# Three narrow matmuls in place of two wide ones for queries, w_o and the first two FFN pairs of a decoder layer

## The chip, the cores and the metric

One of the cores of a Trainium2 chip runs the whole program. The metric is the device time of one execution in microseconds (us); the time before is the median of three runs. The profile is of one execution, and its times count from the start of its span.

## What is computed

One decoder layer on 256 positions of width 2048, in float32: a Mamba-2 SSD mixer, then cross-attention with 4 heads into 256 memory tokens, then a gated FFN with a causal convolution of 3 taps, each between two RMS norms and added to the residual. What matters here, cut from the reference:

```python
q = (h @ w_q).reshape(bsz, L, XA_HEADS, XA_HEAD_DIM)
k, v = jnp.split(mem_n @ w_kv, 2, axis=-1)
...
s = jnp.einsum('bthd,bmhd->bhtm', q, k).astype(jnp.float32) * (XA_HEAD_DIM ** -0.5)
p = jax.nn.softmax(s, axis=-1).astype(v.dtype)
o = jnp.einsum('bhtm,bmhd->bthd', p, v).reshape(bsz, L, XA_DIM)
return o @ w_o
...
u = _causal_dwconv(h @ w_up, conv_w, conv_b)
gate, val = jnp.split(u, 2, axis=-1)
return (jax.nn.silu(gate) * val) @ w_down
```

## The kernel before

Activations lie transposed: 128 channels on the partitions, 256 positions (T) along the row. A float32 product is made of fp32r matmuls on operands split into a high part (a rounded copy, ScalarE, line 139 for weights) and a low part (the rest, VectorE, line 153 for weights): high by high, high by low, low by high. Weights come in chunks of 128 x 2048 through 3 raw buffers, and are split in halves of 1024 columns into 5 split buffers ("split"); a few halves of the first FFN chunks go into free parts of the tile G.

A product of one 128-column block of weights with an activation goes over 16 steps of 128 channels (4 steps for w_o, whose depth is the 4 heads). A step has two forms:

- narrow, `mm3` (lines 241 to 244): three matmuls of 256 columns into the same 256 columns of a PSUM bank;
- wide, `mm2` (lines 246 to 249): the high weights by high and low activations in one matmul of 512 columns, and the low weights by the high activations into the second half of the bank. The block's result is then the sum of the bank's halves: `folded` (lines 251 to 256) copies the second half to SBUF on ScalarE (line 254) and adds the first on VectorE (line 255).

The SSD input projections (80 blocks) are narrow; all from w_out on is wide. After the SSD output the work is laid out in slots, one or more blocks ("lanes") each, in the order: keys 0 to 3, values 0 to 2, queries 0 to 3, value 3, then w_o (16 blocks; the first four as four lanes of one slot, step by step), then the FFN. A block's bank is emptied by its post function in the next slot (`q_post` line 771, `wo_post` line 877, `fconv` line 904), and hooks put the attention between the steps of the slots after: scores of head h (`s_mm`), softmax (`smax`), transposed probabilities (`p_tr`), product with values (`o_mm`), its split into the high and low parts that w_o reads (`o_post`). The tiles q, p and pT have one buffer each, so a head waits for the head before. Banks named pj rotate through four.

`wo_post` squares a block for the third norm, scales it into m, and adds the square to a running sum. When w_o is done, `chain3` (line 983) takes the norm: `pe1` (line 300, matmuls with ones), a power on GpSimd, `pe2` (line 320, transposes), then the residual and the high and low parts of H, which the FFN reads. The first FFN slot has four lanes (gate 0, value 0, gate 1, value 1, in two banks pj and the banks pt and py); their posts are kept ("late") until the fourth norm's row rb is copied (line 328), in the next slot.

The instructions are issued through a scheduler that reorders them on each engine; `hot` raises a post's priority, and `pinned` keeps chain3 in its written order (line 53).

Of the kernel before, what the change touches and what calls it, by code (L numbers as in the profile page):

```python
# [7 lines left out]
F32 = mybir.dt.float32  # L8
FR = mybir.dt.float32r
I32 = mybir.dt.int32  # L10
AF = mybir.ActivationFunctionType
OP = mybir.AluOpType

T = 256
DM = 2048
KD = DM // 128
# [6 lines left out]
NF = FH // 128  # L23
# [38 lines left out]
def hybrid_layer_kernel(ctx, tc, xT, memT, pvd, alog, w_dt, w_in, w_kv, w_q, w_out, w_o, w_up, w_dn, out):  # L62
    nc = tc.nc
    V, S, P, PE = nc.vector, nc.scalar, nc.gpsimd, nc.tensor
# [11 lines left out]
    m = consts.tile([128, KD, T], F32, name="m")  # L76
# [9 lines left out]
    def col(name, j):  # L86
        return pv[:, PV[name] + j:PV[name] + j + 1]
# [4 lines left out]
    B = {}  # L92
# [106 lines left out]
    def hot(fn):  # L199

        def steps(g):
            while True:
                with tc.high_priority():
                    if next(g, g) is g:
                        return
                yield

        def f(*args):
            with tc.high_priority():
                g = fn(*args)  # L210
            return steps(g) if hasattr(g, "__next__") else g
        return f
# [5 lines left out]
    slots = []  # L218

    def new_chunk(src, n, kind="w"):  # L220
        chunks.append((src, n, kind))
        return len(chunks) - 1

    def slot():
        slots.append(Slot())
        return len(slots) - 1
# [3 lines left out]
    def sl(i):  # L230
        return hooked.setdefault(i, Slot())

    def add_block(src, n, mov, post, lane_of=None):

        s = slot() if lane_of is None else lane_of
        c = new_chunk(src, n)
        slots[s].lanes.append((c, 0, mov, post, None, True))
        return s


# [10 lines left out]
    def folded(ps, pool, name, bufs):  # L251

        t = pool.tile([128, T], F32, name=name, bufs=bufs)
        S.activation(t, ps[:, T:], AF.Copy)  # L254
        V.tensor_tensor(t, ps[:, :T], t, op=OP.add)  # L255
        return t

    def hilo(dst, src, scale=None):

        hi, lo = dst  # L260
        if scale is None:
            S.activation(hi, src, AF.Copy)  # L262
            yield
            return V.tensor_tensor(lo, src, hi.bitcast(F32), op=OP.subtract)  # L264
        else:
            S.activation(hi, src, AF.Copy, scale=scale)
            yield
            return V.scalar_tensor_tensor(lo, src, scale, hi.bitcast(F32), op0=OP.mult, op1=OP.subtract)
# [5 lines left out]
    def halves(t):  # L274
        return t[:, 0:T], t[:, T:2 * T]
# [73 lines left out]
    movG = [G[:, k] for k in range(GS)]  # L349
    movH = [H[:, k] for k in range(KD)]  # L350
# [278 lines left out]
    for kind, i in order:  # L629
        s = pos[kind, i]  # L630
        if kind in ("C", "B"):
            blk = 32 + (8 if kind == "C" else 0) + i
# [113 lines left out]
    def v_post(h):  # L746
        def post(ps):
            wB = B["wB"]
            t = folded(ps, wB, "ev", 2)
            V.tensor_tensor(t, t, B["nm"].rbc, op=OP.mult)  # L750
            B["vT", h] = t
        return post

    def k_post(h):
        def post(ps):
            t = folded(ps, B["wB"], "ev", 2)
            V.tensor_tensor(t, t, B["nm"].rbc, op=OP.mult)
            yield from hilo(halves(B["K"][:, h]), t)
        return post
# [11 lines left out]
    def q_post(h):  # L771
        def post(ps):
            q = B["wB"].tile([128, 2 * T], FR, name="q", bufs=1)
            yield from hilo(halves(q), folded(ps, B["wB"], "ev", 2))
            B["q", h] = q
        return post

# [66 lines left out]
    at = {}  # L844
    for kind, h in (("k", 0), ("k", 1), ("k", 2), ("k", 3), ("v", 0), ("v", 1), ("v", 2), ("q", 0), ("q", 1), ("q", 2), ("q", 3), ("v", 3)):
        if kind == "k":
            at[kind, h] = add_block(w_kv[h], 2048, movH, k_post(h))
        elif kind == "v":
            at[kind, h] = add_block(w_kv[XH + h], 2048, movH, v_post(h))
        else:  # L850
            at[kind, h] = add_block(w_q[h], 2048, movG, q_post(h))
    s_k0, s_q0, s_wo = at["k", 0], at["q", 0], max(at.values()) + 1

    hook(s_k0, "pe", lambda: B["nm"].pe1(), 2)
# [11 lines left out]
    for h in range(XH):  # L866
        s = at["q", h]
# [9 lines left out]
    def wo_post(j):  # L877
        def post(ps):
            wB = B["wB"]
            sq = wB.tile([128, T], F32, name="accB" if j == 0 else "sqB", bufs=2 if j else 1)  # L880
            if j == 0:
                B["n3"] = Norm(wB, DM)
            t = folded(ps, wB, "ev", 2)
            B["hold_s"] = S.activation(sq, t, AF.Square)
            S.activation(m[:, j], t, AF.Copy, scale=col("post", KD + j))
            yield
            B["hold_v"] = B["n3"].add(sq, last=j == KD - 1) or B.get("hold_v")
        return post
# [8 lines left out]
    for j in range(KD):  # L897
        if j % 4 == 0:
            c = new_chunk(w_o[j // 4], 2048)
        s = s_wo if 0 < j < 4 else slot()  # L900
        slots[s].lanes.append((c, 4 * (j % 4), MovO(), hot(wo_post(j)), None, True))


    def fconv(ps, blk, dst_name, silu):
        wB = B["wB"]
        t = folded(ps, wB, "ev", 2)
        V.tensor_tensor(t, t, B["n4"].rbc, op=OP.mult)
        u = wB.tile([128, T], F32, name="fu", bufs=2)
        w = PV["fw"] + 3 * blk
        S.activation(u, t, AF.Identity, bias=col("fb", blk), scale=pv[:, w + 2:w + 3])  # L910
        yield
        for j in (1, 0):
            d = 2 - j
            V.scalar_tensor_tensor(u[:, d:], t[:, :T - d], pv[:, w + j:w + j + 1], u[:, d:],  # L914
                                   op0=OP.mult, op1=OP.add)
        if silu:
            s = wB.tile([128, T], F32, name="sg", bufs=2)
            S.activation(s, u, AF.Silu)
            return s
        return u  # L920

    def gate_post(f):
        def post(ps):
            B["gate", f] = yield from fconv(ps, f, "sg", True)
        return post

    def val_post(f):
        def post(ps):
            u = yield from fconv(ps, NF + f, "uv", False)
            V.tensor_tensor(u, u, B.pop(("gate", f)), op=OP.mult)  # L930
            yield from hilo(halves(G[:, f % GS]), u)
        return post
# [20 lines left out]
    up_no = 0  # L953
    first_up = len(slots)

    def add_up(f):
        nonlocal up_no
        if f < 2:
            if f == 0:
                slot()  # L960
                B["late"] = []
                in_g.update({len(chunks): 0, len(chunks) + 1: 1})
                c = len(chunks)
                held.update(range(c, c + 4))
                for i, (dc, h) in enumerate(((0, 0), (0, 1), (1, 0), (2, 0), (3, 0), (1, 1), (2, 1), (3, 1))):
                    moved[c + i // 2, i % 2] = (c + dc, h)
            add_block(w_up[up_no], 2048, movH, lambda ps: B["late"].append((gate_post(f), ps)), lane_of=first_up)
            add_block(w_up[up_no + 1], 2048, movH, lambda ps: B["late"].append((val_post(f), ps)), lane_of=first_up)
        else:
            add_block(w_up[up_no], 2048, movH, gate_post(f))  # L970
            add_block(w_up[up_no + 1], 2048, movH, val_post(f))
        up_no += 2
# [3 lines left out]
    for si, (f0, f1) in enumerate(SETS):  # L976
        while done < min(f1 + 1, NF):
            add_up(done)
            done += 1
        for j in range(KD):  # L980
            add_block(w_dn[si][j], (f1 - f0) * 128, [G[:, f % GS] for f in range(f0, f1)], dn_post(si, j))
# [62 lines left out]
    for i, s in enumerate(slots):  # L1044
# [29 lines left out]
        for k in range(nk):  # L1074
            for ln, ps in zip(lanes, pss):
# [4 lines left out]
                c, off, mov = ln[0], ln[1], ln[2]  # L1080
# [5 lines left out]
                n = len(mov)  # L1086
# [15 lines left out]
    n5, wB = B["n5"], B["wB"]  # L1102
# [99 lines left out]
```

## Time and profile before

| | |
|---|---|
| median of 3 runs | 1584.14 us (1583.5 to 1584.51) |
| the profiled execution: its own time | 1584.14 us |
| its span, first to last instruction | 1582.4 us |
| TensorE (PE) busy | 1543.2 us, 98% |
| VectorE (DVE) busy | 1213.8 us, 77% |
| ScalarE (ACT) busy | 975.9 us, 62% |
| mean granted TensorE clock | 0.991 |

PE is busy in nearly all of the 40 slices of the span; two slices around 780 and 820 us are at 8 and 6 tenths. Matmuls are pipelined and overlap in the records, so what one costs is read from the distance of starts, not from its length. The profile's rows name a line, an engine, an operation, the tile written and the tiles read, and in brackets the idle time before it and what ended it.

### The profile page before, as it was taken

The numbers are of one execution on the slowest core, as the hardware profiler recorded it, in microseconds if no ns is written. First come the engines' busy times: TensorE is split into PE (matmuls) and PEld (weight loads), VectorE is DVE, ScalarE is ACT, GpSimd is POOL, SyncE is SP. The second block draws the span as 40 slices with busy tenths as digits, with TensorE's granted clock in tenths as the row PEclk, the third lists the DMA queues.
The fourth block names the chain that finished last, engine by engine and source line by source line (L and its number), as shares of the span: only waits on it lengthen the run. The fifth ranks groups of instructions, "written<-read, shape, count | busy, mean of one in ns | idle before, by whom it ended". The sixth has DMA issues, their size and how long they took to land.

```text
span 1582.4 us, 25562 instructions
## 1 busy us (share of the span) xinstructions
PE 1543.2 (98%) x10104; PEld 1406.7 (89%) x10104; DVE 1213.8 (77%) x1942; ACT 975.9 (62%) x1603; POOL 7.9 (0%) x14
## 2 busy tenths in 40 slices
PE   8999999999999999999869999999999999999997
PEld 7999999889999999888758788888888888888886
DVE  7799988746898897869578878755877765778775
ACT  6798887645777765756575655544555533555553
POOL 0000000000000000000000000000000000000000
PEclk9999999999999999999989999999999999999999
DMA  7665555554555445754334455555555555555452
GB/s 266 222 219 191 178 194 189 187 195 166 205 180 183 170 160 188 291 177 169 106 107 171 171 191 186 178 197 188 193 195 193 180 186 195 188 190 195 155 208 77
DMA packets 47289, 292.08 MB, mean 185 GB/s; under 512 B 5504, under 2 KB 5568, under 8 KB 19776
## 3 DMA queue, kind: packets, MB, share of 16 engines
q1 hardware_dynamic: 46592, 289.60, 52.6%
q8 instruction: 79, 1.29, 0.3%
q10 hardware_dynamic: 576, 0.84, 0.2%
q14 instruction: 42, 0.34, 0.1%
HBM read 288.26 MB, written 2.16 MB: 184 GB/s over the span
## 4 chain that ended last, share of the span: by engine, by line
PE 51%; issue 45%; DVE 2%; ACT 1%; DMA 1%; POOL 0%; SPq 0%; POOLq 0%; DVEq 0%
PE pj L248 12%; PE pj L244 9%; PE pj L243 9%; PE pj L242 9%; PE pj L249 6%; PE py L244 1%; PE py L242 1%; PE py L243 1%; PE pt L534 0%; DMA m<-in_xT_dram 0%; DVE m L1119 0%; PE ms L300 0%; DMA raw<-in_w_up_dram 0%; ACT hi L139 0%; PE pt L248 0%
## 5 line engine op out<-in xcount | busy, mean ns | idle before, releaser
L139 ACT ACTIVATE hi<-raw 128x1024 fp32r<-128x1024 f32 (+2 forms) x518 | 539.7, 1045 | 481.0 <-PE pj L248 399.2
L153 DVE TENSOR_TENSOR lo<-raw,hi 128x1024 fp32r<-128x1024 f32 (+2 forms) x518 | 623.9, 1206 | 260.8 <-ACT hi L139 256.4
L248 PE MATMUL pj<-H,hi 128*128 128x512 f32 x1472 | 513.0, 393 | 3.4 <-DVE ev L255 3.4
L248 PE MATMUL pj<-G,hi 128*128 128x512 f32 x1280 | 444.5, 392 | 0.0
L249 PE MATMUL pj<-H,lo 128*128 128x256 f32 x1472 | 412.2, 280 | 0.0
L242 PE MATMUL pj<-H,hi 128*128 128x256 f32 x1280 | 361.3, 283 | 6.9 <-ACT hi L262 6.6
L244 PE MATMUL pj<-H,lo 128*128 128x256 f32 x1280 | 360.1, 282 | 0.8 <-DVE lo L264 0.7
L243 PE MATMUL pj<-H,hi 128*128 128x256 f32 x1280 | 360.2, 282 | 0.0
L249 PE MATMUL pj<-G,lo 128*128 128x256 f32 x1280 | 356.7, 280 | 0.0
L248 PEld LDWEIGHTS pj<-H,hi 128*128 128x128 f32 x1472 | 277.0, 188 | 64.6 <-issue 3.7
L248 PEld LDWEIGHTS pj<-G,hi 128*128 128x128 f32 x1280 | 239.8, 188 | 52.1
L249 PEld LDWEIGHTS pj<-H,lo 128*128 128x128 f32 x1472 | 277.1, 188 | 0.1
L242 PEld LDWEIGHTS pj<-H,hi 128*128 128x128 f32 x1280 | 241.4, 189 | 8.8 <-ACT hi L262 7.6
L244 PEld LDWEIGHTS pj<-H,lo 128*128 128x128 f32 x1280 | 241.7, 189 | 2.1 <-DVE lo L264 1.6
L243 PEld LDWEIGHTS pj<-H,hi 128*128 128x128 f32 x1280 | 242.0, 189 | 1.0
L249 PEld LDWEIGHTS pj<-G,lo 128*128 128x128 f32 x1280 | 240.4, 188 | 0.6
L914 DVE SCALAR_TENSOR_TENSOR fu<-ev,pv,fu 128x255 f32<-128x255 f32 (+1 forms) x176 | 84.3, 480 | 3.2 <-ACT fu L910 0.3
L456 DVE SCALAR_TENSOR_TENSOR u<-ev,pv,u 128x255 f32<-128x255 f32 (+2 forms) x144 | 68.5, 478 | 5.1 <-ACT u L452 3.9
L910 ACT ACTIVATE fu<-ev,pv 128x256 f32<-128x256 f32 x88 | 51.7, 589 | 1.1 <-DVE G L264 0.9
L255 DVE TENSOR_TENSOR ev<-pj,ev 128x256 f32<-128x256 f32 x113 | 46.6, 418 | 4.3 <-ACT ev L254 4.3
L254 ACT ACTIVATE ev<-pj 128x256 f32<-128x256 f32 x113 | 40.8, 367 | 7.4 <-PE pj L249 4.7
L367 DVE TENSOR_TENSOR ev<-pj,rx 128x256 f32<-128x256 f32 x80 | 33.6, 421 | 13.2 <-PE pj L244 10.4
(254 smaller groups left out, 1246.1 us busy)
## 6 DMA issues: line engine op xcount, KB each, us to landing
raw<-in_w_up_dram SPq DMA_DIRECT2D x88, 1024.0 KB, 4.8
raw<-in_w_in_dram SPq DMA_DIRECT2D x78, 1024.0 KB, 4.8
raw<-in_w_out_dram SPq DMA_DIRECT2D x32, 1024.0 KB, 4.8
raw<-in_w_dn_dram SPq DMA_DIRECT2D x32, 960.0 KB, 4.7
raw<-in_w_dn_dram SPq DMA_DIRECT2D x16, 896.0 KB, 4.6
rows<-rows_d SPq DMA_DIRECT2D x32, 256.0 KB, 3.9
raw<-in_w_kv_dram SPq DMA_DIRECT2D x8, 1024.0 KB, 4.8
raw<-in_w_q_dram SPq DMA_DIRECT2D x4, 1024.0 KB, 4.8
```

The source lines that it names most:

```text
L139: S.activation(hi_t[c, h][:, :b - a], raw_t[c][:, a:b], AF.Copy)
L153: V.tensor_tensor(lo_t[c, h][:, :b - a], raw_t[c][:, a:b], hi_t[c, h][:, :b - a].bitcast(F32), op=OP.subtract)
L242: PE.matmul(ps, whi, xhi, start=start, stop=False)
L243: PE.matmul(ps, whi, xlo, start=False, stop=False)
L244: B["mm"] = PE.matmul(ps, wlo, xhi, start=False, stop=stop)
L248: PE.matmul(ps, whi, x, start=start, stop=False)
L249: B["mm"] = PE.matmul(ps[:, T:], wlo, x[:, 0:T], start=False, stop=stop)
L254: S.activation(t, ps[:, T:], AF.Copy)
L255: V.tensor_tensor(t, ps[:, :T], t, op=OP.add)
L456: V.scalar_tensor_tensor(u[:, d:], ps[:, :T - d], pv[:, w + j:w + j + 1], u[:, d:], op0=OP.mult, op1=OP.add)
L910: S.activation(u, t, AF.Identity, bias=col("fb", blk), scale=pv[:, w + 2:w + 3])
L914: V.scalar_tensor_tensor(u[:, d:], t[:, :T - d], pv[:, w + j:w + j + 1], u[:, d:], op0=OP.mult, op1=OP.add)
```

## The change

Queries, w_o and the first two FFN pairs (gates and values 0 and 1) go back from the wide to the narrow form; keys, values, all other FFN blocks, and the SSD output stay wide. Their posts read the bank directly instead of a folded tile: `q_post` splits it, `wo_post` squares it and scales it (the scaling of every fourth block goes to VectorE), and `fconv` multiplies it by the norm's row.

```diff
-    def add_block(src, n, mov, post, lane_of=None):
+    def add_block(src, n, mov, post, lane_of=None, wide=True):
...
-        slots[s].lanes.append((c, 0, mov, post, None, True))
+        slots[s].lanes.append((c, 0, mov, post, None, wide))
...
-            yield from hilo(halves(q), folded(ps, B["wB"], "ev", 2))
+            yield from hilo(halves(q), ps[:, :T])
...
-            at[kind, h] = add_block(w_q[h], 2048, movG, q_post(h))
+            at[kind, h] = add_block(w_q[h], 2048, movG, q_post(h), wide=False)
...
-            t = folded(ps, wB, "ev", 2)
-            B["hold_s"] = S.activation(sq, t, AF.Square)
-            S.activation(m[:, j], t, AF.Copy, scale=col("post", KD + j))
+            B["hold_s"] = S.activation(sq, ps[:, :T], AF.Square)
+            if j % 4:
+                S.activation(m[:, j], ps[:, :T], AF.Copy, scale=col("post", KD + j))
+            else:
+                V.tensor_scalar(m[:, j], ps[:, :T], col("post", KD + j), None, op0=OP.mult)
...
-        slots[s].lanes.append((c, 4 * (j % 4), MovO(), hot(wo_post(j)), None, True))
+        slots[s].lanes.append((c, 4 * (j % 4), MovO(), hot(wo_post(j)), None, False))
...
-        t = folded(ps, wB, "ev", 2)
-        V.tensor_tensor(t, t, B["n4"].rbc, op=OP.mult)
+        if blk % NF < 2:
+            t = wB.tile([128, T], F32, name="ev", bufs=2)
+            V.tensor_tensor(t, ps[:, :T], B["n4"].rbc, op=OP.mult)
+        else:
+            t = folded(ps, wB, "ev", 2)
+            V.tensor_tensor(t, t, B["n4"].rbc, op=OP.mult)
...
-            add_block(w_up[up_no], 2048, movH, lambda ps: B["late"].append((gate_post(f), ps)), lane_of=first_up)
-            add_block(w_up[up_no + 1], 2048, movH, lambda ps: B["late"].append((val_post(f), ps)), lane_of=first_up)
+            add_block(w_up[up_no], 2048, movH, lambda ps: B["late"].append((gate_post(f), ps)), lane_of=first_up, wide=False)
+            add_block(w_up[up_no + 1], 2048, movH, lambda ps: B["late"].append((val_post(f), ps)), lane_of=first_up, wide=False)
```

The scheduler also orders the engines anew. ScalarE from the first query's split to the first softmax, before (q is a query's split, ev a fold's copy, hi a weight split, p the exponentials):

```order
L262 ACTIVATE q<-ev 128x256
L139 ACTIVATE hi<-raw 128x1024
L254 ACTIVATE ev<-pj 128x256
L139 ACTIVATE hi<-raw 128x1024
L262 ACTIVATE q<-ev 128x256
L139 ACTIVATE hi<-raw 128x1024
L254 ACTIVATE ev<-pj 128x256
L805 ACT_TABLE_LOAD
L805 ACTIVATE p,sm<-py,mx,sr 128x256 x2
```

and now (Vt is the split of a transposed value block, which in the order before stands earlier):

```order
L262 ACTIVATE q<-pj 128x256
L139 ACTIVATE hi<-raw 128x1024
L262 ACTIVATE Vt<-pt 128x256
L139 ACTIVATE hi<-raw 128x1024 x2
L262 ACTIVATE q<-pj 128x256
L262 ACTIVATE Vt<-pt 128x256
L805 ACT_TABLE_LOAD
L805 ACTIVATE p,sm<-py,mx,sr 128x256 x2
```

The copies are gone, and the softmax stands before the fourth value's fold. On PE the scores of head 0 stood behind 9 steps of value 3's block, and now stand in query 3's block, around its sixth to ninth step.

ScalarE at the end of w_o, before (the posts of blocks 13 to 15: the rows of line 53 are those of block 15):

```order
L139 ACTIVATE hi<-raw 128x1024
L884 ACTIVATE sqB<-ev 128x256
L885 ACTIVATE m<-ev,pv 128x256
L254 ACTIVATE ev<-pj 128x256
L139 ACTIVATE hi<-raw 128x1024
L884 ACTIVATE sqB<-ev 128x256
L885 ACTIVATE m<-ev,pv 128x256
L53 ACTIVATE ev<-pj 128x256
L53 ACTIVATE sqB<-ev 128x256
L53 ACTIVATE m<-ev,pv 128x256
```

and now:

```order
L139 ACTIVATE hi<-raw 128x1024
L883 ACTIVATE sqB<-pj 128x256
L885 ACTIVATE m<-pj,pv 128x256
L883 ACTIVATE sqB<-pj 128x256
L885 ACTIVATE m<-pj,pv 128x256
L53 ACTIVATE sqB<-pj 128x256
L53 ACTIVATE m<-pj,pv 128x256
```

A post has two instructions on ScalarE instead of three (one, in every fourth block), nothing waits for VectorE between them, and one weight split now stands behind block 15's post.

VectorE at the late posts of the first two FFN pairs, before (rb is the fourth norm's row, fu the convolution):

```order
L153 TENSOR_TENSOR lo<-raw,hi 128x1024 x3
L328 COPY rb<-ms 128x256
L907 TENSOR_TENSOR ev<-ev,rb 128x256 x2
L153 TENSOR_TENSOR lo<-raw,hi 128x1024
L914 SCALAR_TENSOR_TENSOR fu<-ev,pv,fu 128x255 x2
L914 SCALAR_TENSOR_TENSOR fu<-ev,pv,fu 128x254 x2
L153 TENSOR_TENSOR lo<-raw,hi 128x1024
L930 TENSOR_TENSOR fu<-fu,sg 128x256
L255 TENSOR_TENSOR ev<-pt,ev 128x256
L255 TENSOR_TENSOR ev<-py,ev 128x256
L907 TENSOR_TENSOR ev<-ev,rb 128x256 x2
```

and now:

```order
L153 TENSOR_TENSOR lo<-raw,hi 128x1024 x2
L328 COPY rb<-ms 128x256
L910 TENSOR_TENSOR ev<-pj,rb 128x256 x2
L153 TENSOR_TENSOR lo<-raw,hi 128x1024
L920 SCALAR_TENSOR_TENSOR fu<-ev,pv,fu 128x255 x2
L920 SCALAR_TENSOR_TENSOR fu<-ev,pv,fu 128x254 x2
L910 TENSOR_TENSOR ev<-pt,rb 128x256
L910 TENSOR_TENSOR ev<-py,rb 128x256
```

The two banks pj of pair 0 were emptied by folds ahead of these rows; now they are read only after the copy of rb. The sums of the folds and two weight splits (one ahead of rb, one behind) have left this stretch.

## Rows read from the trace of the kernel before

**Rows 1.** The page, busy time by engine over the span
```profile
PE 1543.2 (98%) x10104; PEld 1406.7 (89%) x10104; DVE 1213.8 (77%) x1942; ACT 975.9 (62%) x1603; POOL 7.9 (0%) x14
```

**Rows 2.** PE's waits, 650 to 860 us: total us, times, longest
```profile
PE ms L300 <- DVE accB L290: 6.8, 1, 6.8
PE pj L248 <- DVE H L53: 3.3, 1, 3.3
PE py L242 <- ACT q L262: 2.7, 1, 2.7
```

**Rows 3.** PE's waits, 845 us to the end
```profile
PE pj L248 <- DVE ev L255: 3.4, 1, 3.4
```

**Rows 4.** Stretches: us, busy PE, PEld, DVE, ACT, POOL, granted clock, DMA share, GB/s
```profile
811.00:826.00 15.00, 2.82 (x11) 2.28 (x11) 10.21 (x21) 8.29 (x17) 1.54 (x1) 0.67 0.41 141
877.00:881.00 4.00, 3.94 (x14) 3.33 (x15) 3.63 (x10) 2.42 (x6) 0.00 (x0) 0.58 0.25 104
```

**Rows 5.** PE's timeline (start us, length us): 13 narrow steps, then 33 wide steps
```profile
28.93 0.28 PE L242 MATMUL pj<-H,hi 128*128 128x256 f32 x1
...
33.56 0.28 PE L242 MATMUL pj<-H,hi 128*128 128x256 f32 x1
...
1000.05 0.39 PE L248 MATMUL pj<-H,hi 128*128 128x512 f32 x1
...
1011.49 0.39 PE L248 MATMUL pj<-H,hi 128*128 128x512 f32 x1
```

**Rows 6.** ACT's timeline: query 0's copy, exponentials of heads 0 and 3
```profile
756.39 0.36 ACT L254 ACTIVATE ev<-pj 128x256 f32<-128x256 f32 x1
...
769.86 0.56 ACT L805 ACTIVATE p<-py,mx,sr 128x256 f32<-128x256 f32 x1
...
782.55 0.56 ACT L805 ACTIVATE p<-ms,mx,sr 128x256 f32<-128x256 f32 x1
```

**Rows 7.** PE's timeline: head 0's scores, w_o, the third norm, the FFN's first matmul
```profile
763.99 0.28 PE L242 MATMUL py<-KT,q 128*128 128x256 f32 x1
...
790.21 0.50 PE L248 MATMUL pj<-KT,hi 128*128 128x512 f32 x1 [0.93 <-DVE KT L264]
...
791.76 0.49 PE L248 MATMUL pj<-KT,hi 128*128 128x512 f32 x1
...
810.64 0.28 PE L249 MATMUL pj<-KT,lo 128*128 128x256 f32 x1
817.75 0.59 PE L300 MATMUL ms<-ones,accB 128*128 128x1 f32 x2 [6.83 <-DVE accB L290]
...
819.40 0.56 PE L300 MATMUL ms<-ones,sqB 128*128 128x1 f32 x2
...
825.90 0.77 PE L248 MATMUL pj<-H,G 128*128 128x512 f32 x1 [3.31 <-DVE H L53]
```

**Rows 8.** Groups by line, 757 to 826 us: xcount, busy us, mean ns
```profile
L885 ACT ACTIVATE m<-ev,pv 128x256 f32<-128x256 f32 x15 | 7.4, 496 | 0.0
L254 ACT ACTIVATE ev<-pj 128x256 f32<-128x256 f32 x19 | 6.4, 370 | 2.2 <-PE pj L249 1.2 <-DVE q L264 1.1
L884 ACT ACTIVATE sqB<-ev 128x256 f32<-128x256 f32 x14 | 5.7, 408 | 2.6 <-DVE ev L255 2.6
```

**Rows 9.** ACT's timeline: block 15's square, the first high part of H
```profile
818.06 0.42 ACT L53 ACTIVATE sqB<-ev 128x256 f32<-128x256 f32 x1 [0.99 <-DVE ev L53]
...
823.54 0.51 ACT L53 ACTIVATE H<-x,pv 128x256 fp32r<-128x256 f32 x1 [3.72 <-DVE x L53]
```

**Rows 10.** DVE's timeline: pair 0 multiplied by rb
```profile
865.00 0.76 DVE L907 TENSOR_TENSOR ev<-ev,rb 128x256 f32<-128x256 f32 x2
```

**Rows 11.** PE's timeline: gate 3's first step, the stall ahead of gate 4, full clock again
```profile
862.18 0.39 PE L248 MATMUL pj<-H,hi 128*128 128x512 f32 x1
...
877.06 0.47 PE L248 MATMUL pj<-H,hi 128*128 128x512 f32 x1 [3.40 <-DVE ev L255]
...
881.13 0.40 PE L248 MATMUL pj<-H,hi 128*128 128x512 f32 x1
```

More of the change, by code (lines that the diff above doesn't have):

```diff
@@ L900, in hybrid_layer_kernel, with fconv @@
         s = s_wo if 0 < j < 4 else slot()
-        slots[s].lanes.append((c, 4 * (j % 4), MovO(), hot(wo_post(j)), None, True))
-    def fconv(ps, blk, dst_name, silu):
+        slots[s].lanes.append((c, 4 * (j % 4), MovO(), hot(wo_post(j)), None, False))
+    def fconv(ps, blk, silu):
         wB = B["wB"]
-        t = folded(ps, wB, "ev", 2)
-        V.tensor_tensor(t, t, B["n4"].rbc, op=OP.mult)
+        if blk % NF < 2:
[4 more added lines that the diff above has]
+            V.tensor_tensor(t, t, B["n4"].rbc, op=OP.mult)
         u = wB.tile([128, T], F32, name="fu", bufs=2)
@@ L923, in post @@
         def post(ps):
-            B["gate", f] = yield from fconv(ps, f, "sg", True)
+            B["gate", f] = yield from fconv(ps, f, True)
         return post
@@ L928, in post @@
         def post(ps):
-            u = yield from fconv(ps, NF + f, "uv", False)
+            u = yield from fconv(ps, NF + f, False)
             V.tensor_tensor(u, u, B.pop(("gate", f)), op=OP.mult)
```

## The prediction
> **What bounds the kernel now.** I read the page's busy times first: PE is busy 98% of the span [rows 1], so elsewhere time comes only from PE work itself. Then PE's waits: the three largest from 650 to 860 us stand around attention, w_o and the third norm [rows 2], and one stands alone in the FFN [rows 3]. The stretch from 811 to 826 us shows what they do: 15 us in which PE works 2.82 [rows 4]. So two questions settle this case: what a narrow step costs on PE, and which of these waits hang on the folds that go.
>
> **Price of a step.** A matmul's length overlaps its neighbours', so starts count. 13 narrow steps take 33.56 - 28.93 = 4.63 us, 0.356 each; 33 wide steps take 1011.49 - 1000.05 = 11.44 us, 0.347 each [rows 5]. A narrow step costs 0.010 us more (0.0095, rounded up). The change makes 4 x 16 steps for queries, 16 x 4 for w_o, and 4 x 16 in the FFN narrow: 192 x 0.010 = **+1.9 us**, all on PE's path. The Trainium skill (TensorE: Matmul & The Clock Gate, "Wait — 56ns, not 53.3ns?") gives a full-clock matmul its columns' time plus some 2.5 ns; by it one more matmul a step would cost 192 x 2.5 ns = 0.5 us, an estimate. The trace's difference is four times that, and the rows decide.
>
> **Queries and attention.** A wide query's way to its scores is a copy on ScalarE, a sum on VectorE, then the split on both, each queued behind weight splits. Query 0's copy starts at 756.39 [rows 6] and head 0's scores only at 763.99 [rows 7], behind 9 steps of value 3. The new order puts the query's split where the copy stood, and the scores into query 3's block: 16 steps earlier, 16 x 0.356 = 5.7 us. PE has work in this stretch anyhow (the rest of the projections), so an earlier head takes time off only if the whole chain of four heads follows. In the order now, I walked it with durations of before. Exponentials of head 0 at 763.6 instead of 769.86, of head 3 at 777.4 instead of 782.55 [rows 6]; then the last head's split, and w_o's fourth step at 785.3 instead of 790.21 [rows 7]. That is 4.9, net of the 0.6 that the queries' narrow steps cost, so 5.5 gross. Several of its hops rest on where PE fits head matmuls between projection steps, so I take **-5.0 us**. The bounds are 0 (heads paced as now, only begun earlier: PE would wait among them instead of ahead of them) and -6.3 (head 0's whole lead kept).
>
> **Posts of w_o.** A block's post now costs ScalarE a copy, a square and a scaling, 370, 408 and 496 ns [rows 8], with VectorE's sum between the first and the second. Starts of neighbours lie some 0.1 closer than these lengths. With the weight splits between them the posts fall behind PE, and banks come free late: 47 steps from 791.76 to the start of the last at about 810.4 [rows 7] take 0.397 each instead of 0.347, 2.4 us too much. Now a post costs ScalarE a square and, in three of four blocks, a scaling: 0.3 + 0.75 x 0.4 = 0.6 us by starts, and the seven weight splits of this stretch add 7 x 0.96 / 16 = 0.42. That is 1.0 us a block against PE's 4 x 0.356 = 1.43. ScalarE keeps up; I leave 0.4 for the first bank: **-2.0 us** (bounds 0 and -2.4).
>
> **The tail.** PE's last w_o matmul starts at 810.64, lasts 0.28, and the third norm's sums wait until 817.75; its last starts at 819.40 [rows 7]. The wait is the backlog: block 15's square runs at 818.06 [rows 9], seven microseconds behind its data. With ScalarE level with PE, the square follows the last matmul by a hop of some 0.2, takes 0.42 [rows 9], and the last sum starts 0.9 behind it (819.40 - 818.06 = 1.3 with the square in it). So 1.6 us from PE's end instead of 819.40 - 810.92 = 8.5: **-6.9 us**. Late next would be the fourth split of FFN weights, which moves behind block 15's post and puts a second low part of 1.2 us ahead of the residual on VectorE; GpSimd's power, which runs at that time (1.54) [rows 4], and the transposes cover it to within some 0.2. Bounds: -3.5 (half the backlog remains) and -7.2.
>
> **The FFN's first matmul.** A wide matmul reads the high and low parts of H together, so it starts at 825.90 [rows 7], though the first high part is there from 823.54 + 0.51 = 824.05 [rows 9]. Four narrow matmuls that need only it can run in that wait. At the half clock (here 1.2 GHz) that PE comes back with, four take about 4 x 0.21: **-0.8 us** (bounds 0 and -1.8).
>
> **The late posts.** Now the folds empty pair 0's banks before rb is known, but two folds, a weight split and more stand ahead of gate 2's fold. So PE stands still for 3.40 us ahead of gate 4, then runs 7 steps in 881.13 - 877.06 = 4.07 us instead of 2.4 [rows 11], at a granted clock of 0.58 [rows 4]: 3.4 + 1.6 = 5.0. In the new order gate 2's fold comes three microseconds earlier by VectorE's durations (two sums, a split, a split's wait), and that stall goes. In its place gate 3 needs a bank that is read only behind rb: PE gets there at 862.18 [rows 11], less one step for the new place of the transposes. Before, rb's first product ran at 865.00 [rows 10] behind a split that is no longer ahead of it. Without that split, transposes at 861.8, copy at 862.3 and product at 862.7 free the bank at 863.2, 1.2 later than PE wants it. Sum **-3.8 us** (bounds +0.5, if rb is as late as now and the clock falls too, and -5.0).
>
> **Sum.** 1.9 - 5.0 - 2.0 - 6.9 - 0.8 - 3.8 = -16.6 us. The profiled execution took 1584.14 us, which is also the median, with 1.7 outside the span. 1584.1 - 16.6 = **1567.5 us**. Everything before query 0 and behind gate 4 keeps its order in kind, and PE its 98%; I cost it at nothing.
>
> **Rivals.**
> - *The heads keep their pace.* One buffer each for q, p and pT ties a head to the one before, and PE's wait for a query's split is only 2.7 us [rows 2]. Without the attention term: 1572.5. For it: the chain is long and has no slack; against it: the softmax of head 0 is moved ahead of value 3's fold. 0.15.
> - *The splits are the backlog, not the folds.* If weight splits and their raw loads hold ScalarE in w_o, half of the tail stays (3.4) and half of w_o's stalls (1): 1572, and 1577 together with the first rival. Against it: ScalarE waited 2.6 us for VectorE's sums at the squares alone [rows 8]. 0.15.
> - *ScalarE becomes w_o's bound: slower.* A bank is read twice now, by square and scaling. The Trainium skill (VectorE: DVE Perf Modes, "Rules for kernel authors") advises for several operations on a matmul's output to copy it to SBUF first, which the change undoes. It decides once posts and splits take more than PE's 1.43 us a block; from there each further 0.1 costs 1.6 over 16 blocks. To use up 16.6 us, a post would need 2.5 us a block, 2.1 without splits, against 0.6; then 1587 to 1590. The copy that reads a bank takes 370 ns, less than the square's 408 from SBUF [rows 8], which speaks against it. 0.04.
> - *More than forecast*, if the clock stays up in places where it now falls, or all bounds meet: 1562. 0.06.
>
> That the narrow form wouldn't be used is excluded by the built order. The forecast itself has 0.60.
>
> **Numbers.** 1567.5 us. The range takes the cases at 1572 and most of the one at 1577, and the lower bounds of single terms: 1563.5 to 1576. 0.2%, about 3.2 us, is what a measurement of this kernel can tell from no change. Faster by more: all cases but the slower rival and a sum where nearly all terms fail: 0.93; within: 0.03; slower: 0.04.
>
> **What would show it.** The wait for the running sum (6.8) under 1.5; exponentials of head 0 some 6 us earlier against the projections; the first FFN matmul narrow and ahead of the low part; no 3.4 wait ahead of gate 4, but one of about 1 ahead of gate 3, for the product with rb. A long wait of PE for ScalarE or VectorE inside w_o, or among the heads, would make it wrong.

## The result and the profile after

The changed kernel takes **1563.98 us** (median; 1563.46 to 1564.14), the kernel before 1583.86 in the same comparison: a ratio of 0.9873, 95% interval 0.9856 to 0.9891. It is faster by 20 us; the time lies 3.5 us below the forecast of 1567.5 and half a microsecond above the lower end of the range, 1563.5 to 1576.

The page of the changed kernel, busy time by engine (the line of [rows 1]):

```profile
PE 1538.6 (99%) x10296; PEld 1413.8 (91%) x10296; DVE 1205.5 (77%) x1922; ACT 967.3 (62%) x1575; POOL 7.9 (1%) x14
```

PE runs 192 matmuls more, is busy 4.6 us less in all, and its share rises to 99%: what went is time in which it stood still or ran slowly. PE's waits from 650 to 860 us, where [rows 2] stood before:

```profile
PE pj L242 <- ACT H L53: 2.7, 1, 2.7
...
PE pj L248 <- DVE ev L910: 1.1, 1, 1.1
PE pj L242 <- ACT KT L262: 0.9, 2, 0.5
PE pj L242 <- DVE mx L802: 0.7, 1, 0.7
...
PE pj L243 <- DVE H L53: 0.5, 1, 0.5
PE pj L242 <- DVE m L887: 0.3, 1, 0.3
```

The wait of 6.8 for the running sum is gone, and so is the 2.7 for a query's split. The wait for H's first high part (2.7) and low part (0.5) is what is left of 3.3; the 1.1 ahead of gate 3 (for the product with rb, L910) is new, and the 3.4 of [rows 3] is not there any more. The first steps of w_o wait twice for the high part of a head's output (the 0.9); from block 4 of w_o on, PE waits once, 0.3.

Two stretches with the columns of [rows 4], around the FFN's first matmul, and from the fourth norm's sums to behind gate 4, whose first step now comes at about 859:

```profile
806.00:816.00 10.00, 7.38 (x38) 7.09 (x39) 9.90 (x20) 6.71 (x12) 0.00 (x0) 0.66 0.39 126
...
840.00:900.00 60.00, 58.93 (x349) 52.02 (x348) 50.96 (x89) 39.25 (x62) 1.54 (x1) 1.00 0.54 183
```

In the second one PE misses only the 1.07 ahead of gate 3, and the clock is full.

PE's timeline, with the places of [rows 7, 11] (start, length, and in brackets the wait ahead): the norm ahead of the queries, head 0's scores, w_o's fourth step and block 4, the last w_o matmul, the third norm's sums, the FFN's first matmul, gate 3:

```profile
700.87 0.28 PE L300 MATMUL ms<-ones,sqB 128*128 128x1 f32 x2
...
757.48 0.28 PE L242 MATMUL py<-KT,q 128*128 128x256 f32 x1
...
783.12 0.38 PE L242 MATMUL pj<-KT,hi 128*128 128x256 f32 x1 [0.47 <-ACT KT L262]
...
785.09 0.39 PE L242 MATMUL pj<-KT,hi 128*128 128x256 f32 x1 [0.28 <-DVE m L887]
...
802.35 0.28 PE L244 MATMUL pj<-KT,lo 128*128 128x256 f32 x1
802.73 0.38 PE L300 MATMUL ms<-ones,accB 128*128 128x1 f32 x2
...
803.57 0.36 PE L300 MATMUL ms<-ones,sqB 128*128 128x1 f32 x2
...
808.14 0.80 PE L242 MATMUL pj<-H,G 128*128 128x256 f32 x2 [2.69 <-ACT H L53]
...
847.77 0.47 PE L248 MATMUL pj<-H,hi 128*128 128x512 f32 x1 [1.07 <-DVE ev L910]
```

ScalarE's timeline, with the places of [rows 6, 9]: query 0's split, now straight from the bank, the exponentials of heads 0 and 3, block 15's square:

```profile
754.80 0.37 ACT L262 ACTIVATE q<-pj 128x256 fp32r<-128x256 f32 x1
...
762.68 0.57 ACT L805 ACTIVATE p<-py,mx,sr 128x256 f32<-128x256 f32 x1
...
776.36 0.56 ACT L805 ACTIVATE p<-ms,mx,sr 128x256 f32<-128x256 f32 x1
...
802.66 0.39 ACT L53 ACTIVATE sqB<-pj 128x256 f32<-128x256 f32 x1 [0.63 <-PE pj L244]
```

Executions differ by up to 1.6 us at the very start. So times are compared behind one row that comes before any changed block, the first residual norm's sums: 700.87 here, and in the kernel before

```profile
700.83 0.28 PE L300 MATMUL ms<-ones,sqB 128*128 128x1 f32 x2
```

Behind that row, in us (the runs are told of below; "end" is the span's):

| kernel | exp. of head 0 | w_o block 4 | last w_o matmul | n3's last sum | first FFN matmul | end |
|---|---|---|---|---|---|---|
| before | 69.03 | 90.93 | 109.81 | 118.57 | 125.07 | 881.57 |
| changed | 61.81 | 84.22 | 101.48 | 102.70 | 107.27 | 861.03 |
| e1, queries wide | 69.03 | 90.53 | 107.79 | 109.01 | 113.58 | 867.52 |
| e2, w_o wide | 61.81 | 84.86 | 103.74 | 112.66 | 117.36 | 870.58 |
| e3, FFN pairs wide | 61.80 | 84.19 | 101.44 | 102.66 | 109.72 | 865.97 |
| e4, narrow, folds kept | 66.30 | 86.88 | 105.90 | 114.61 | 119.30 | 876.62 |
| e5, wide, no folds | 65.99 | 86.37 | 103.00 | 104.33 | 110.62 | 863.13 |
| e10, queries narrow, folds | 66.30 | 86.84 | 105.74 | 114.58 | 121.08 | 876.92 |
| e11, w_o narrow, folds | 69.03 | 90.12 | 109.13 | 117.95 | 124.36 | 880.65 |
| e12, order alone | 66.34 | 89.12 | 108.00 | 116.78 | 123.28 | 879.98 |

So 6.7 us come up to w_o's block 4, 1.6 in w_o, 7.5 in the tail, 1.9 at the FFN's first matmul, and 2.7 behind it: 20.5 between these two executions, 19.9 between the medians. One of e1's four executions took 5404 us in a slow state; the time given for e1 is the median of the other three.

### The profile page after: what moved, and what is told of

Same layout as the page of the kernel before. It is cut to its first block, busy times and chain, and to the rows that moved or that the text cites. A ratio compares the mean times of both kernels' runs of the same rounds, so it can differ in the third digit from the quotient of the medians.

```text
span 1561.9 us, 25901 instructions
## 1 busy us (share of the span) xinstructions
PE 1538.6 (99%) x10296; PEld 1413.8 (91%) x10296; DVE 1205.5 (77%) x1922; ACT 967.3 (62%) x1575; POOL 7.9 (1%) x14
## 4 chain that ended last, share of the span: by engine, by line
PE 51%; issue 45%; DVE 2%; ACT 1%; DMA 0%; POOL 0%; SPq 0%; POOLq 0%; DVEq 0%
PE pj L242 11%; PE pj L244 11%; PE pj L243 11%; PE pj L248 10%; PE pj L249 5%; PE py L244 1%; PE py L243 1%; PE py L242 1%; PE pt L534 0%; DMA m<-in_xT_dram 0%; DVE m L1125 0%; PE ms L300 0%; DVE xacc L290 0%; PE pt L243 0%; PE pt L244 0%
## 5 line engine op out<-in xcount | busy, mean ns | idle before, releaser
L248 PE MATMUL pj<-G,hi 128*128 128x512 f32 x1216 | 421.9, 392 | 0.0
L249 PE MATMUL pj<-G,lo 128*128 128x256 f32 x1216 | 339.3, 280 | 0.0
L248 PEld LDWEIGHTS pj<-G,hi 128*128 128x128 f32 x1216 | 228.0, 188 | 49.9
L249 PEld LDWEIGHTS pj<-G,lo 128*128 128x128 f32 x1216 | 228.3, 188 | 0.4
L255 DVE TENSOR_TENSOR ev<-pj,ev 128x256 f32<-128x256 f32 x92 | 38.6, 420 | 0.0
L262 ACT ACTIVATE Mh<-dec 128x768 fp32r<-128x768 f32 x32 | 27.0, 843 | 16.3 <-PE py L244 15.5
```

Of the source, the lines that this page charges most:

```text
L248: PE.matmul(ps, whi, x, start=start, stop=False)
L249: B["mm"] = PE.matmul(ps[:, T:], wlo, x[:, 0:T], start=False, stop=stop)
```

## The experiments

Theory A is the prediction's: the time came from the folds' hops between PE and the next user of the data. Theory B: the narrow form itself, or the new order, gave it. Theory C: the groups are coupled, and one's gain is soaked up by the next.

**One group undone at a time (e1, e2, e3).** From the changed kernel, one group gets back its wide blocks and folds:

```diff
# e1
-            yield from hilo(halves(q), ps[:, :T])
+            yield from hilo(halves(q), folded(ps, B["wB"], "ev", 2))
...
-            at[kind, h] = add_block(w_q[h], 2048, movG, q_post(h), wide=False)
+            at[kind, h] = add_block(w_q[h], 2048, movG, q_post(h))
```

That is e1. In e2, wo_post has its fold, square and scaling of before, and w_o's lanes are wide; in e3, fconv folds every block, and both blocks of pairs 0 and 1 are wide.

Expected of e1:

> The changed kernel with the four query blocks wide and folded again, w_o and the two FFN pairs left narrow. Theory A (the time came from the folds' hops between PE and the next user of the data, group by group): the 6.7 us by which the w_o stage began earlier in the trace of the change come back and nothing else moves, so 1564.0 + 6.7 = 1570.7 us; the scores of head 0 start near 764 instead of 757.5, and the granted clock falls again among the heads. Theory B (the narrow form itself, or the new order that the scheduler made of everything, gave the time): the queries are a third of the narrow steps, so about a third of 20, or less: 1564 to 1570, with the scores of head 0 still near 757.5. Theory C (the groups are coupled: a late w_o start is soaked up by w_o's own waits): under 1567.

Expected of e2:

> The changed kernel with w_o wide and folded again, queries and the two FFN pairs left narrow. Theory A: w_o's 1.6 us net and the third norm's 7.5 us come back, 1564.0 + 9.1 = 1573.1 us; the third norm's sums again wait for the running sum, some 6 to 7 us in one wait. Theory B: a third of 20 or less, with that wait staying under 2 us. Theory C: the backlog is made in the w_o stage by the attention's late start; with the heads early, half of the wait at most, so 1568 to 1570.

Expected of e3:

> The changed kernel with the first two FFN pairs wide and folded again, queries and w_o left narrow. Theory A: between the third norm's last sum (15.8 us ahead of the kernel before) and the end (20.5 ahead) lies 4.7 us, and that comes back: 1568.7 us; the stall of 3.4 us ahead of gate 4 and the half clock behind it are there again. Theory B: up to a third of 20, 1570, or nothing, without that stall. Theory C: the stall ahead of gate 4 hung on late splits of w_o's stage; with those early it stays away, and only the 0.8 to 1.9 us of the FFN's first matmul come back, 1565 to 1566.

Measured: e1 1570.43 (0.9913, interval 0.9897 to 0.9930), e2 1573.25 (0.9933, 0.9918 to 0.9948), e3 1568.04 (0.9899, 0.9885 to 0.9914). Against 1563.98 that is 6.45 for the queries, 9.27 for w_o with its tail and 4.06 for the FFN pairs. They add up to 19.8, the whole difference to within the scatter of single executions (about 1 us), so the groups are not coupled: C falls. The table agrees: in e1 everything behind the heads is the changed kernel's, 6.3 to 6.5 later. The waits come back one by one: in e1 the query's 2.7, and the granted clock from 772 to 779 us is 0.50; in e2 the running sum's, in e3 the one ahead of gate 4.

```profile
772.00:779.00 7.00, 6.17 (x27) 5.47 (x27) 4.75 (x14) 2.87 (x8) 0.00 (x0) 0.50 0.00 0
```
```profile
PE ms L300 <- DVE accB L290: 7.0, 1, 7.0
```
```profile
PE pj L248 <- DVE ev L255: 3.4, 1, 3.4
```

**Form and fold apart (e4, e5).** e4 keeps the narrow form and both instructions of the fold; e5 keeps the short posts and makes the matmuls wide.

```diff
+    def refolded(ps, pool, name, bufs):
+        t = pool.tile([128, T], F32, name=name, bufs=bufs)
+        S.activation(t, ps[:, :T], AF.Copy)
+        V.tensor_tensor(t, ps[:, :T], t, op=OP.max)
+        return t
```

e4 calls this in the posts of all three groups. e5 has only wide set to True in them: PE computes the second half of the bank, and nothing reads it, so e5 leaves one product out of its result.

Expected of e4:

> The narrow form in all three groups as in the change, but with the fold's two instructions kept as they were: ScalarE copies the bank's half to SBUF, VectorE takes the maximum of that copy and the same half (the same values), and the rest of the post reads the result. So only PE's work and what can start without the low parts differ from the kernel before. Theory A: nearly all the gain is gone and the narrow steps' 1.9 us are to be paid; the FFN's first matmul still can start early (0.8 to 1.9): 1584 to 1586 us, with the long wait for the running sum (6 to 7 us) back. Theory B (the narrow form or the order gives the time): 1564 to 1570. If half of the gain stayed, 1574, the folds would be one cause among two.

Expected of e5:

> The changed kernel with its short posts, but with the wide matmuls back in queries, w_o and the two FFN pairs. The bank's second half, which holds the high weights times the low moving part, is computed by PE and never read, so that product is left out of the output. With the run that kept the folds this makes a square of two by two: form (wide or narrow) and post (folded or direct). Theory A (the folds' hops are the cause): 1564.0, less the narrow steps' 1.9, plus the 1.9 that the FFN's first matmul waits for its low part, so 1562 to 1566 us. Theory D (form and folds are two separate causes that add up, as 1578.1 with folds kept in the narrow form could be read): the 6.0 us that the narrow form kept go, 1564.0 + 6.0 = 1570 us. If the result is near A, the 6 us are something that either of the two removes.

Measured: e4 1578.11 (0.9963, 0.9951 to 0.9976), e5 1566.04 (0.9884, 0.9869 to 0.9898). So the narrow form alone gives 6.0 us, the missing folds alone 18.3, and both 19.9: the folds are the main cause, and e4 fits neither theory, since 6.0 stay where A expected nothing and B all. PE's waits in e4 (650 to 900 us; the helper shifts its lines by 7), then in e5:

```profile
PE ms L307 <- DVE accB L297: 6.8, 1, 6.8
PE pj L248 <- DVE ev L255: 3.0, 1, 3.0
```
```profile
PE pj L248 <- DVE H L53: 4.2, 1, 4.2
...
PE pj L248 <- DVE ev L910: 1.1, 1, 1.1
...
PE ms L300 <- DVE accB L290: 0.4, 1, 0.4
```

With folds the running sum's wait and the stall ahead of gate 4 are there in either form; without them they are gone in either form. For w_o, the tail and the late posts this is theory A. (The place of the weight splits changes with the folds, and the runs do not hold the two apart there.) The FFN's first matmul goes by the form: from n3's last sum to it 4.6 us in the changed kernel, 4.7 in e4, but 6.3 in e5, which waits for H's low part. The attention goes by neither alone: up to block 4 of w_o, e4 is 4.05 ahead of before, e5 4.56, and the changed kernel, which has both, 6.71. Theory A had expected nothing of the narrow form there.

**What the narrow queries do (e10, e11).** From the kernel before, queries alone, or w_o alone, narrow with the fold of e4.

Expected of e10:

> The kernel before, with the queries alone narrow and their fold kept (copy and maximum of the same half), w_o and the FFN as before. If the 4.0 us by which the w_o stage began earlier in the run with all folds kept come from the narrow queries (their order against the splits and the scores), 1584.1 - 4.0 = 1580 us, with the exponentials of head 0 near 767 instead of 770. If they come from w_o's high products, which can run among the heads while the low parts of the attention's output are still made, this kernel only pays 64 x 0.010 = 0.6: 1584.7 us, with the exponentials near 770.

Expected of e11:

> The kernel before, with w_o alone narrow and its fold kept, queries and FFN as before: the counterpart of the run on the queries. If the 4.0 us come from w_o's high products among the heads, about 1580 us; if from the queries, 1584.1 + 0.6 = 1584.7 us. In both cases the wait for the running sum stays at 6 to 7 us, since the folds of w_o stay.

Measured: e10 1579.08 (0.9969, 0.9957 to 0.9981), e11 1582.72 (0.9991, 0.9981 to 1.0001; its interval takes in no change). e10 reaches block 4 as early as e4 does, so it is the queries; e11 gains 0.8 up to there, where its narrow w_o steps start on the high part of the attention's output (below). Here is ScalarE in e10 (L261 copies query 0's bank, L269 splits it; the norm's row stands at 700.48):

```profile
753.44 2.01 ACT L139 ACTIVATE hi<-raw 128x1024 fp32r<-128x1024 f32 x2 [3.75 <-PE pj L243]
755.36 0.36 ACT L269 ACTIVATE Vt<-pt 128x256 fp32r<-128x256 f32 x1
755.62 0.38 ACT L261 ACTIVATE ev<-pj 128x256 f32<-128x256 f32 x1
755.88 1.06 ACT L139 ACTIVATE hi<-raw 128x1024 fp32r<-128x1024 f32 x1
758.00 1.06 ACT L139 ACTIVATE hi<-raw 128x1024 fp32r<-128x1024 f32 x1 [1.06 <-PE pj L243]
758.97 0.40 ACT L269 ACTIVATE q<-ev 128x256 fp32r<-128x256 f32 x1
...
765.07 0.40 ACT L269 ACTIVATE q<-ev 128x256 fp32r<-128x256 f32 x1
765.48 1.28 ACT L812 ACT_TABLE_LOAD   x1
766.78 0.57 ACT L812 ACTIVATE p<-py,mx,sr 128x256 f32<-128x256 f32 x1
```

The instructions are those of before; two weight splits stand between the copy and the split of query 0 where before there were three. Behind the norm's row the split of the high part runs 0.7 us earlier (58.49 against 59.20), head 0's first score matmul 1.6 (61.57 against 63.16), and its exponentials 2.7: on ScalarE a weight split and a query's copy stood between query 1's split and the exponentials, and now, as the last rows show, nothing but the table load does.

**The order alone (e12).** The kernel before, all wide and folded, with value 3's weight splits issued behind query 0's split:

```diff
+    held.update([slots[at["v", 3]].lanes[0][0]])
```

Query 0's post sets B["hold_s"] and B["hold_v"] to the two instructions of its split, and what is held is issued behind them.

> The kernel before, with all blocks wide and all folds kept as they are, and one thing in another order: the splits of value 3's weights are issued behind query 0's split on ScalarE and VectorE, instead of ahead of it. In the order this puts query 0's split right behind its fold and the scores of head 0 into query 3's block, as in the change. Narrow queries with their folds kept, and wide queries without folds, each gave most of the attention's gain; if what both do is to change that place in the queues, this kernel gains too: exponentials of head 0 before 767 instead of 769.9, the w_o stage 3 to 5 us earlier, so 1579 to 1581 us against 1584.1. If the gain needs less work on ScalarE and VectorE, or the narrow form on PE, the heads catch up nothing or value 3 waits for its weights: 1583.5 to 1586.

Measured: 1581.44 (0.9982, 0.9973 to 0.9991), less than expected. ScalarE in e12 (norm's row at 699.52) splits query 0 right behind its copy, and the weights later:

```profile
754.24 0.38 ACT L254 ACTIVATE ev<-pj 128x256 f32<-128x256 f32 x1 [2.86 <-PE pj L249]
755.11 0.42 ACT L776 ACTIVATE q<-ev 128x256 fp32r<-128x256 f32 x1 [0.49 <-DVE ev L255]
755.44 1.99 ACT L139 ACTIVATE hi<-raw 128x1024 fp32r<-128x1024 f32 x2
```

Head 0's exponentials are as early as in e10 (66.34 and 66.30 behind the norm), with no instruction changed: the order in the queues is a cause. But block 4 gains only 1.8 of e10's 4.1. PE waits 1.65 us for the softmax's product of head 0 in e12, ahead of head 2's scores; e10 waits 1.14 for the same product, ahead of head 0's transposes. After it e12 runs at the half clock and e10 does not. The two waits, e12's first, and the stretch from 772 to 779 us in e12, in the kernel before, in the changed one and in e10 (columns of [rows 4]):

```profile
768.36 0.39 PE L242 MATMUL py<-KT,q 128*128 128x256 f32 x1 [1.65 <-DVE p L818]
```
```profile
769.28 0.72 PE L828 MATMUL ms<-ident,p 128*128 128x128 f32 x4 [1.14 <-DVE p L817]
```
```profile
772.00:779.00 7.00, 6.04 (x31) 5.10 (x29) 4.82 (x16) 2.51 (x8) 0.00 (x0) 0.68 0.00 0
```
```profile
772.00:779.00 7.00, 6.17 (x26) 5.43 (x27) 4.75 (x13) 2.85 (x9) 0.00 (x0) 0.53 0.00 0
```
```profile
772.00:779.00 7.00, 5.94 (x43) 5.33 (x44) 5.46 (x17) 3.56 (x11) 0.00 (x0) 1.00 0.00 1
```
```profile
772.00:779.00 7.00, 5.84 (x40) 4.92 (x40) 5.75 (x16) 4.37 (x13) 0.00 (x0) 1.00 0.00 0
```

The clock alone seems cheap here: e4 ran four microseconds of the heads at 0.57, e10 the same heads at full clock, and block 4 starts within 0.04 of each other, though e4's narrow w_o steps may have made up for some of it, by e11 up to 0.8. How the remaining 2.3 us divide between clock and the order of heads 2 and 3 stays open.

**The price of a step (e6, e7).** e6 makes the other 84 FFN up blocks narrow with direct posts; e7 does the opposite to the 32 z blocks of the input projection.

```diff
-            S.activation(t, x_scaled(ps), AF.Silu)
+            e = folded(ps, wA, "ev", 2)
+            V.tensor_tensor(e, e, x_norm.rbc, op=OP.mult)
+            S.activation(t, e, AF.Silu)
```

That is e7's post, and its lanes are wide. In e6, fconv multiplies every block straight from the bank, and every add_block of the pairs has wide=False.

Expected of e6:

> The changed kernel with all 84 remaining FFN up blocks narrow too and their product with rb read straight from the bank: the price of a narrow step by itself, in a stage where PE waits for nothing, so that no fold's way can pay for it. 84 x 16 = 1344 steps: at 0.0095 us a step (before's pitch) +12.8, so 1576.8 us; at 2.5 ns for the one more matmul, as the Trainium skill's page on TensorE's matmul and clock gate has it, +3.4, so 1567.4 us. If shorter posts helped even here, less than either.

Expected of e7:

> The changed kernel with the 32 z blocks of the input projection, which are narrow in both kernels, made wide and folded: the opposite edit, in a stage where PE waits for nothing. If only the step's price counts: 32 x 16 = 512 steps at the 5.5 ns that all FFN up blocks narrow cost a step (7.4 us over 1344), so -2.8: 1561.2 us. If VectorE, busy for 131 of 150 us there, becomes PE's bound by the added sums (0.42 x 32 = 13 us over 500), PE waits appear in the trace between 30 and 600 us and the time is over 1566.

Measured: e6 1571.42 (0.9915, 0.9900 to 0.9930), 7.4 above the changed kernel, or 5.5 ns a step: neither 9.5 nor 2.5. Its trace shows 118 narrow steps without a gap at 0.3519 each; e1's w_o, narrow as well and without a wait, shows 45 steps at 0.3600:

```profile
1104.22 0.28 PE L242 MATMUL pj<-H,hi 128*128 128x256 f32 x1
...
1145.75 0.28 PE L242 MATMUL pj<-H,hi 128*128 128x256 f32 x1
```
```profile
792.33 0.28 PE L242 MATMUL pj<-KT,hi 128*128 128x256 f32 x1
...
808.53 0.28 PE L242 MATMUL pj<-KT,hi 128*128 128x256 f32 x1
```

e7 1564.40 (0.9880, 0.9863 to 0.9896): no gain. Two waits that the changed kernel does not have, 3.4 us together, eat the 2.8, the first for an x block's product from the bank, the second for a split of x:

```profile
PE pj L248 <- DVE ev L367: 2.1, 1, 2.1
PE py L244 <- DVE xdr L264: 1.3, 1, 1.3
```

**Around w_o (e8, e9).** e8 makes value 3 narrow with a direct post; e9 gives ScalarE the scaling of every fourth w_o block as well.

```diff
-            t = folded(ps, wB, "ev", 2)
-            V.tensor_tensor(t, t, B["nm"].rbc, op=OP.mult)
+            t = wB.tile([128, T], F32, name="ev", bufs=2)
+            V.tensor_tensor(t, ps[:, :T], B["nm"].rbc, op=OP.mult)
```

This is e8's post for the last value; e9 drops the branch on j % 4 in wo_post.

Expected of e8:

> The changed kernel with value 3's block narrow too and read straight from the bank. It is the one folded block left between the queries and w_o. If a fold among the heads still holds the last head, the w_o stage begins 0.5 to 1.5 us earlier: 1562.5 to 1563.5 us. If the heads' own chain sets it, only the steps are paid: 16 x 0.006 = 0.1, so 1564.1 us.

Expected of e9:

> The changed kernel with the scaling of every fourth w_o block on ScalarE too, instead of VectorE. It adds 4 x 0.36 us to ScalarE in the w_o stage. If ScalarE has room there, as the sum had it (1.0 us of work a block against PE's 1.43), the time stays within 0.5 of 1564.0, and the third norm's last sum starts within 0.5 us of the change's, counted from the last w_o matmul. If ScalarE were at its limit, the third norm's sums start 1 us or more later and the time is 1565 or more.

Measured: e8 1563.03 (0.9868, 0.9853 to 0.9883), with block 4 of w_o 0.6 us earlier (83.7 behind the norm); the best time seen, but its interval covers the changed kernel's ratio. e9 1563.71 (0.9872, 0.9857 to 0.9886), with n3's last sum 1.2 us behind the last w_o matmul, as in the change: ScalarE has room in w_o.

## Why the prediction was right, step by step

- **Price of a step, +1.9.** Wrong as one price. The forecast took 0.0095 us from 13 steps at the kernel's start; the same form costs 0.0053 in the FFN (0.3519 against 0.3466 for 121 wide steps of the changed kernel there) and 0.0133 in w_o (0.3600). For 64 steps each that is 0.3 and 0.9; the queries' price was not measured by itself, and at these two prices the sum is 1.5 to 2.0, so its size is about right. The Trainium skill's 2.5 ns per matmul, there for matmuls back to back (TensorE: Matmul & The Clock Gate, "Wait — 56ns, not 53.3ns?") is not what these rows show for one matmul more; in the FFN they give twice that, in w_o five times.
- **Queries and attention, -5.0.** The term that was too small. Undoing the queries costs 6.5 net, against 4.4 net forecast (-5.0 and 0.6). The walk took durations of before, where the granted clock from 772 to 779 us was 0.53; it is 1.00 now. It missed at two hops. Head 0's exponentials were put at 763.6 and run at 762.68; head 3's follow, 777.4 and 776.36. From there to w_o's fourth step it took the 7.7 of before and a little more; it is 6.8, since PE waits twice 0.47 there for a high part (as at 783.12 above), where a wide step waited twice 0.93 for the low one ([rows 7] at 790.21). That is w_o's narrow form at work, 0.8 by e11, 0.6 by e2 and 0.4 by e1. And the cause was too narrow: the attention's gain does not need the folds gone. The narrow form (e10), the missing fold (e5) and an order written by hand (e12) all bring head 0's exponentials forward by 2.7 to 3.0. In each the scheduler's order changes: query 0's split stands ahead of more weight splits (of all three in e5 and e12, of one in e10), and in e10 the exponentials stand ahead of one more as well. The two first together bring 7.2.
- **Posts of w_o, -2.0.** Block 4 to the last matmul took 18.9 before and 17.3 now; with 48 steps at 0.0133 added back, 2.3. ScalarE keeps up, as worked out: 2.1 of the 2.8 us that it waits there are for PE.
- **The tail, -6.9.** It is 7.5: from the last w_o matmul to the last sum 8.8 before, 1.2 now. e4 and e5 tie it to the folds and not to the form.
- **The FFN's first matmul, -0.8.** It starts 1.9 closer to the third norm, and all of that is given back: 0.5 for the first low part, narrow steps, and 6.1 us at the half clock (808.14 to 814.28) instead of 3.8 (825.90 to 829.67). From n3's last sum to the fourth norm's sums (841.62, 857.13 before) it is 38.1 against 37.7, and one more step of gate 2 and value 2 stands ahead of these sums now (21 instead of 20), 0.3 us: net, nothing was gained.
- **The late posts, -3.8.** From the fourth norm's sums to the end 720.3 against 725.3: 5.0, and 4.6 without that one step, between the forecast and its lower bound. The new stall ahead of gate 3 is 1.1 where 1.2 was forecast.
- **The sum.** Net of the narrow steps the five stages gave 6.7, 1.6, 7.5, 0.0 and 4.6 us, where 4.4, 1.4, 6.9, 0.2 and 3.8 were forecast. The folds' hops are the mechanism in w_o, the tail and the late posts, as forecast, and one of two in the attention; the range held only narrowly, and more than half of the miss is the attention's.
- **The rivals.** Heads that keep their pace, splits as the backlog, and ScalarE as w_o's bound did not come. "More than forecast" came in part: the clock stayed up among the heads, as it had been named, though what that gave was not measured by itself. The advice in the third rival, from the Trainium skill (VectorE: DVE Perf Modes, "Rules for kernel authors"), to copy a matmul's output to SBUF for many operations, does not pay here for two operations on ScalarE: square and scaling straight from the bank take 394 and 486 ns in this group view of ScalarE (757 to 806 us), the two from SBUF took 408 and 496 [rows 8], and the copy is saved.

```profile
L883 ACT ACTIVATE sqB<-pj 128x256 f32<-128x256 f32 x14 | 5.5, 394 | 2.4 <-PE pj L244 1.5 <-ACT m L885 0.7
L885 ACT ACTIVATE m<-pj,pv 128x256 f32<-128x256 f32 x11 | 5.3, 486 | 0.0
```

## What to carry to other kernels

A form that saves PE time per step but lengthens the post is worth it only where PE never waits for that post; at stage ends and in short dependent chains the post's hops cost far more than the steps save (18.3 us in e5 against some 2 here). Where an in-order queue holds both long background splits and a short split on the path, look at how many stand ahead of the short one. The scheduler may move it when the form of another instruction changes, so the order of the changed kernel is to be read, not derived.

## What the runs showed that was not expected

The same narrow step, at the full clock and without waits, takes 0.352 us in the FFN, 0.356 at the kernel's start and 0.360 in w_o, while the wide one takes 0.347 in the FFN and in w_o (e5: 45 steps from 788.24 to 803.84). What slows three narrow matmuls there and not two wide ones stays open. The clock was not foreseen either: e4 and e10 show the same three waits of PE among the heads (1.14, 0.45 and 0.25 us, all 0.9 later in e10), and then the granted clock fell to its lower level in e4 and stayed up in e10:

```profile
770.00:774.00 4.00, 3.75 (x18) 3.58 (x18) 3.66 (x12) 1.90 (x7) 0.00 (x0) 0.57 0.00 0
```
```profile
770.00:774.00 4.00, 2.94 (x18) 2.06 (x17) 3.91 (x10) 3.00 (x9) 0.00 (x0) 1.00 0.15 64
```

So which of the two a stretch gets could not be read from its waits.
